# Two attention parts of a head pair placed by position over a whole period, and a PSUM bank for one of them

## The chip, the core and the metric

The kernel runs on one core of a Trainium2 chip, in one launch. The metric is the device time of that core in microseconds (us), the median of several runs. The engines are TensorE (PE, matmuls; its weight loads are shown as PEld), VectorE (DVE), ScalarE (ACT), GpSimd (POOL) and SyncE (SP), from which every DMA of this kernel is issued. Matmul results land in PSUM, which here is cut into eight banks of 128 x 512 fp32.

## What is computed

One step of a hybrid decoder layer, for 1024 prompt positions and 32 sample rows (8 requests of 4 tokens):

```python
z = rms_norm(x) @ w_in                       # 1056 x 2048 by 2048 x 7168
q, k, v, ga, u, vc, gb = split(z)            # 16 heads x 64; three gates and u, vc of width 1024
q, k = rope(q), rope(k)
oa = sum of three dilated windows of softmax attention, (128,1), (512,4), (2048,16), merged by denominators
vc = layer_norm(gelu(vc)); oc = gelu(u) * (masked 128x128 mixing of vc per group + bias)
y = rms_norm(x + concat(oa * silu(ga), oc * silu(gb)) @ w_out)
```

The prompt attends to itself; the sample attends to a cache of 2048 past positions, of which 896 per request are needed, and to its own 4 tokens. Keys, values and the normalised vc rows are outputs too.

## The kernel before, in words

**Precision.** Every fp32 operand of a matmul is split into a high and a low fp16 half (`hilo`, line 145; `w_split` for weights), and a product is three matmuls: high by high, high by low, low by high. So ACT makes each high half and DVE each low one.

**Projections.** The input projection has 56 tiles of 128 output columns, the output projection 16. A tile is 16 blocks of 128 deep, by three products, by three chunks of 352 rows: 144 matmuls on PE (`proj_chunk`, line 173). Its PSUM tiles come from the pool `ps_p` with three banks. A tile's weights are loaded two tiles ahead (`w_load`) and split one tile ahead, in four parts.

**Periods.** A head pair p needs the tiles v (values), x and y (queries and keys, whose two halves `rope` turns; `run_ab` runs both tiles chunk by chunk), g (its gate), and the loop adds u and b of the chunk group. Period p, from 1 to 8, is the run of tiles `g, u, b, v, x, y`: it has six tiles for p = 2 to 5 and five for p = 1, 6, 7 and 8. In it the projections of pair p run, and beside them the attention of pair g = p - 1.

**Steps beside a tile.** `proj_chunk` calls `fill` after every six matmuls: 24 calls a tile (`CALLS`). `fill` takes steps from a queue of (cost, function) and keeps their summed costs in proportion to the calls. A step only issues instructions; they go into the engines' streams there, and the scheduler of the language moves some of them by its own reckoning. Four lists of steps exist: the split of the next weights; `prompt_steps`; `sample_steps`; `mix_steps` (the chunk mixing).

**Prompt attention**, 16 items (8 query blocks by 2 heads), in 20 slots. Slot s issues for item s the scores (`fa`: PE into a bank of `ps_s`, a custom DVE reduce that adds the mask and finds the row's minimum, ACT's exp), for item s-1 the two halves of the probabilities (`fb`: ACT, DVE, and one DMA transpose on SP for each of up to two pieces, pn to pt), for item s-3 the product with the values (`fc`: PE into a bank of `ps_o`, then ACT and DVE), and in every second slot the gate (`gate`: a PE transpose into `ps_t`, then DVE and ACT).

**Sample attention**, per request (batch) a `prep` for keys and one for values: a load of 448 KB on SP into one of two buffers kvr, its high half kvh (ACT for keys, POOL for values), its low half kvl (DVE). `s_new` and `s_mm` are the scores: 7 key blocks by 2 small matmuls a batch. `soft1` transposes them in two groups of four blocks, each into its own `bank(ps_t)`, with the same custom reduce after each, then exp, sum and halves; it takes two of the three pn buffers. `soft2` transposes the probabilities by DMA (pst). `pv_new` and `pv_mm` are the products with the values, 14 small matmuls a batch, in one bank of `ps_o`. `fin` gates and stores the pair's result.

**Where they stand before.** The prompt's list is cut into pieces for the tiles g, u, b and v; the sample's first two loads are at the end of b's list, and all the rest of the sample runs beside x and y (in period 8 beside u and b of the last group). `wait(c)` is an empty step that only holds the queue back.

**PSUM before**: `ps_p` three banks, `ps_s` two, `ps_t` two, `ps_o` one. `ps_s` also takes the sample's scores, `ps_t` every PE transpose and the mixing (`mix`, whose result stays in its bank until DVE has made the low half chl), `ps_o` the sample's products.

Of the kernel before, what the change touches and what calls it, by code (L numbers as in the profile page):

```python
# [17 lines left out]
DB = 8  # L18
# [5 lines left out]
NP = H // 2  # L24
# [30 lines left out]
def hybrid_step_kernel(  # L55
# [40 lines left out]
    ps_s = pool("ps_s", bufs=2, space=PSUM)  # L96
    ps_t = pool("ps_t", bufs=2, space=PSUM)
    ps_o = pool("ps_o", bufs=1, space=PSUM)
# [6 lines left out]
    def bank(p, tag):  # L105
        return p.tile([128, 512], F32, tag=tag, name=tag)


# [44 lines left out]
    def set_steps(steps, ncalls):  # L153
# [5 lines left out]
        prog[2] = 0.0  # L159

    def fill():
# [105 lines left out]
    def x_tr(i, qd):  # L267
        t0, n = TILES[i]
        t = xn[i]
        p = bank(ps_s if qd % 2 else ps_t, "s" if qd % 2 else "t")  # L270
# [29 lines left out]
    def vc_sample(m0):  # L300
        p = bank(ps_t, "t")
        for j in range(4):
# [246 lines left out]
    def run_ab(p, steps):  # L549
        a, b = MA[p], MB[p]  # L550
        set_steps(steps, 2 * CALLS)
        for ci, (c0, n) in enumerate(CHUNKS):
# [6 lines left out]
            with tc.high_priority(offset=150):  # L559
                rope(p, pa, pb, c0, n)  # L560
        drain()
        stack_load()

# [31 lines left out]
    def prompt_steps(p):  # L595
# [91 lines left out]
        for s in range(n + 4):  # L687
            fs = []
            cost = 1.2 if s > 4 else 2.0
            if s - 4 >= 0 and (s - 4) % 2 == 1:  # L690
                fs.append(lambda t=(s - 4) // 2: gate(t))
            if 0 <= s - 3 < n:
                fs.append(lambda i=s - 3: fc(i))
                cost += 0.04 * (items[s - 3][0] + 1)
            if 0 <= s - 1 < n:
                fs.append(lambda i=s - 1: fb(i))
            if s < n:
                fs.append(lambda i=s: fa(i))
                cost += 0.04 * (items[s][0] + 1)
            slots.append((cost, lambda fs=fs: [f() for f in fs]))  # L700
        return slots, ahl

    def sample_steps(p, ahl):
# [97 lines left out]
        def pv_new():  # L801
            o = bank(ps_o, "o")
            cur["o"] = o
# [38 lines left out]

        pre = [(0.05, lambda: load(0)), (0.05, lambda: load(1))]
        s1 = [(0.1, lambda: prep(0)), (0.1, lambda: prep(1)), (0.2, s_new), wait(0.8)]
# [6 lines left out]
        return pre, s1, s2  # L851

# [71 lines left out]

    def cut(steps, fr):
        tot = sum(c for c, _ in steps)
        out, i, acc = [], 0, 0.0
        for f in fr:
            cur = []
            while i < len(steps) and (acc + steps[i][0] * 0.5 < f * tot or f >= 1.0):  # L930
                cur.append(steps[i])
                acc += steps[i][0]
                i += 1
            out.append(cur)
        return out

    def act_load(kts, c0, n):
# [4 lines left out]

    def head_start(pr):
        return [wait(1.5)] + pr

    def tail(p, steps):
        w_load(MB[p] + 1)
        for part in range(4):
            w_split(MB[p], part)
        run_ab(p, steps)  # L950

    for p in range(1, NP + 1):
        g = p - 1
        pr, ahl = prompt_steps(g)
        pre, s1, s2 = sample_steps(g, ahl)
        vs = lambda: spread(v_trs(p), 3)
        if p < NP - 2:
            mix_load(g)
            a2, a3, a4 = cut(pr[5:], (0.33, 0.67, 1.0))
            if g > 0:  # L960
                run_m(MG[g], head_start(pr[:5]), ga_evac)
            else:
                a2 = head_start(pr[:5]) + a2
            run_m(MU[g], a2, u_evac)
            run_m(MGB[g], a3 + pre, gb_evac)
            run_m(MV[p], merge(a4, mix_steps(g)), v_evac(p))
            tail(p, merge(s1 + s2, vs()))
        elif p == NP - 2:
            a2, a3 = cut(pr[5:], (0.5, 1.0))
            run_m(MG[g], head_start(pr[:5]), ga_evac)  # L970
            run_m(MU[g], a2 + pre, u_evac)
            run_m(MV[p], a3, v_evac(p))
            tail(p, merge(s1 + s2, vs()))
        elif p == NP - 1:
            mix_load(g - 1)
            a2, a3 = cut(pr[5:], (0.5, 1.0))
            run_m(MG[g], head_start(pr[:5]), ga_evac)
            run_m(MGB[g - 1], a2 + pre, gb_evac)
            run_m(MV[p], merge(a3, mix_steps(g - 1)), v_evac(p))
            tail(p, merge(s1 + s2, vs()))  # L980
        else:
            mix_load(g - 1)
            a2, a3, a4 = cut(pr[5:], (0.45, 0.9, 1.0))
            run_m(MG[g], head_start(pr[:5]), ga_evac)
            run_m(MU[g - 1], a2, u_evac)
            run_m(MGB[g - 1], a3 + pre, gb_evac)
            m = MU[g]
            w_load(m + 2)
            set_steps(mix_steps(g - 1) + merge(a4 + s1, split_steps(m + 1)), CALLS)
            for c0, n in CHUNKS:  # L990
                u_evac(proj_chunk(m, c0, n), c0, n)
            drain()
            mix_load(g)
            m = MGB[g]
            w_load(m + 2)
            set_steps(merge(s2, split_steps(m + 1)), CALLS)
            for ci, (c0, n) in enumerate(CHUNKS):
                gb_evac(proj_chunk(m, c0, n), c0, n)
                if ci == 2:
                    drain()  # L1000
                act_load(slice(0, 7), c0, n)
                act_load(slice(8, 15), c0, n)
            for c0, n in CHUNKS:
                act_load(slice(7, 8), c0, n)
            last_mix = mix_steps(g, direct=True)

# [53 lines left out]
    def ys_tr(m):  # L1060
        p = bank(ps_t, "t")
        PE.transpose(p[0:NS, 0:128], yts.pop(m), eye_t)  # L1062
# [3 lines left out]
    def y_tr(m, t0, w, sample=False):  # L1066
        p = bank(ps_t, "t")
        n = NS if sample else 128
# [230 lines left out]
```

## Time and profile before

| | |
|---|---|
| median of 3 runs | 1881.85 us (1880.05 to 1886.13) |
| the profiled execution: its own time | 1881.56 us |
| its span in the profile | 1879.8 us |
| granted clock of TensorE, mean | 0.995 |
| PE busy | 1790.0 us, 95% of the span |
| DVE, ACT, POOL busy | 58%, 39%, 7% |

A row of waits reads: engine, tile and line that waited, what it waited for, us in total, times, longest. A row of windows gives each engine's busy time and count in a stretch of the span, then the granted clock (1.00 is full), the DMA share and the rate. A row of the timeline gives start, duration, engine, line, operation, output and inputs. A row of a group gives the count, the busy time and the mean ns, then the idle time before it. The first period begins at 301.2 us and the last input tile ends at 1515.9 us.

### The profile page before, as it was taken

Reading aid. Unit: us, or ns where it says so; the run is one execution under the profiler, and the core shown is the slowest. Engines: PE = TensorE matmul, PEld = TensorE weight load, DVE = VectorE, ACT = ScalarE, POOL = GpSimd, SP = SyncE. Lnnn points to the kernel's source line nnn. Section 1 sums busy time; section 2 is a strip of 40 time slices with the busy share of each in tenths; the row PEclk is TensorE's granted clock in tenths of the full one; section 3 lists DMA queues with packets and bytes.
Section 4 is the critical chain, followed back from the end, with each engine's and each line's share of the span. In section 5 each row is a group of like instructions: output and inputs, shape, how many; then the busy total and the mean of one; then the engine's idle time right before and its main releaser. Section 6 shows DMA issues by size and latency. Waiting matters only on the chain. (4 is left out here: it accounts for less than half of the span.)

```text
span 1879.8 us, 37188 instructions
## 1 busy us (share of the span) xinstructions
PE 1790.0 (95%) x15040; PEld 1220.3 (65%) x15040; DVE 1085.5 (58%) x2392; ACT 724.5 (39%) x1605; POOL 125.2 (7%) x139
## 2 busy tenths in 40 slices
PE   8999998999999999999999999999989999999997
PEld 7866665666666666666666656666656666666667
DVE  7733696746665665665755566566566533324344
ACT  7522323632542453354244245245245311212134
POOL 0000010001001000100100100100100110000001
PEclk9999999999999999999999999999999999999999
DMA  7433346666656655656665666576675697222324
GB/s 260 118 81 68 81 135 184 122 166 172 147 117 180 180 120 162 191 115 154 172 157 125 160 202 116 149 210 130 165 197 110 178 336 190 68 68 68 77 59 185
DMA packets 340414, 276.13 MB, mean 147 GB/s; under 512 B 255889, under 2 KB 291729, under 8 KB 338129
## 3 DMA queue, kind: packets, MB, share of 16 engines
q1 hardware_dynamic: 340242, 273.76, 56.3%
q8 instruction: 117, 1.92, 0.4%
q14 instruction: 55, 0.45, 0.1%
HBM read 179.85 MB, written 38.26 MB: 116 GB/s over the span
## 5 line engine op out<-in xcount | busy, mean ns | idle before, releaser
L181 PE MATMUL proj<-xh,wh 128*128 128x352 f16 (+3 forms) x3712 | 1107.7, 303 | 6.2 <-DVE ta L475 2.9
L181 PE MATMUL proj<-xl,wh 128*128 128x352 f16 (+3 forms) x3712 | 1107.3, 303 | 1.5 <-DVE xl L147 1.5
L181 PE MATMUL proj<-xh,wl 128*128 128x352 f16 (+3 forms) x3712 | 1107.1, 303 | 0.4 <-DVE wl L139 0.4
L181 PEld LDWEIGHTS <-wh 128*128 128x128 f16 x7424 | 696.9, 98 | 325.4 <-issue 6.0
L181 PEld LDWEIGHTS <-wl 128*128 128x128 f16 x3712 | 362.6, 98 | 169.7 <-issue 1.9
L139 DVE SCALAR_TENSOR_TENSOR wl<-wraw,wh 128x512 f16<-128x512 f32 x288 | 202.3, 730 | 124.8 <-ACT wh L138 123.9
L138 ACT ACTIVATE wh<-wraw 128x512 f16<-128x512 f32 x288 | 165.8, 620 | 205.7 <-PE proj L181 198.7
L723 DVE SCALAR_TENSOR_TENSOR kvl<-kvr,kvh 128x896 f16<-128x896 f32 x128 | 143.0, 1117 | 95.3 <-ACT kvh L720 53.0
L632 ACT ACTIVATE sp<-sp,mn 128x256 f32<-128x256 f32 (+7 forms) x128 | 99.0, 773 | 150.6 <-DVE mn L620 150.6
L147 DVE SCALAR_TENSOR_TENSOR pn<-sp,pn 128x512 f16<-128x512 f32 (+2 forms) x192 | 106.4, 565 | 33.5 <-ACT pn L146 32.7
L722 POOL TENSOR_SCALAR kvh<-kvr 128x896 f16<-128x896 f32 x64 | 70.2, 1098 | 439.6 <-DMA kvr<-in_vc 272.2
L146 ACT ACTIVATE pn<-sp 128x512 f16<-128x512 f32 (+2 forms) x192 | 94.8, 516 | 11.4 <-DMA pt<-pn 8.4
L720 ACT ACTIVATE kvh<-kvr 128x896 f16<-128x896 f32 x64 | 60.7, 948 | 80.7 <-DMA kvr<-in_kc 46.4
L620 DVE CUSTOM_DVE_ANT_0 sp<-s,mp 128x512 f32<-128x512 f32 (+3 forms) x128 | 74.3, 584 | 21.6 <-PE s L612 20.1
L659 PE MATMUL o<-vst,pt 128*128 128x128 f16 x576 | 66.5, 220 | 21.0 <-DMA pt<-pn 17.4
L147 DVE SCALAR_TENSOR_TENSOR yhl<-proj,yhl 128x352 f16<-128x352 f32 (+1 forms) x42 | 21.4, 510 | 92.3 <-ACT yhl L146 92.3
L146 ACT ACTIVATE yhl<-proj 128x352 f16<-128x352 f32 (+1 forms) x42 | 18.8, 448 | 135.9 <-PE proj L181 116.5
L659 PEld LDWEIGHTS <-pt 128*128 128x128 f16 x576 | 52.1, 98 | 28.5 <-DMA pt<-pn 18.5
L639 DVE RECIPROCAL r<-den 128x1 f32<-128x1 f32 x128 | 20.8, 162 | 81.1 <-ACT sp L632 80.9
L666 PE MATMUL o<-vst,pt 128*128 128x64 f16 x576 | 63.0, 193 | 0.0
L923 POOL TENSOR_TENSOR gb<-gb,tb 128x352 f32<-128x352 f32 x24 | 28.8, 1201 | 511.4 <-DVE tb L203 511.4
L611 PE MATMUL s<-khd,qst 128*128 128x512 f16 (+2 forms) x192 | 61.7, 327 | 0.9 <-DVE mn L620 0.9
(165 smaller groups left out, 1562.6 us busy)
## 6 DMA issues: line engine op xcount, KB each, us to landing
wraw<-in_w_in SPq DMA_DIRECT2D x110, 512.0 KB, 4.5
kvr<-in_kc SPq DMA_DIRECT2D x64, 448.0 KB, 4.3
kvr<-in_vc SPq DMA_DIRECT2D x64, 448.0 KB, 4.0
wraw<-in_w_out SPq DMA_DIRECT2D x32, 512.0 KB, 5.1
yn<-in_x SPq DMA_DIRECT2D x8, 1024.0 KB, 9.2
out_y_p<-yn SPq DMA_DIRECT2D x16, 512.0 KB, 3.5
xn<-in_x SPq DMA_DIRECT2D x7, 1024.0 KB, 6.4
out_v_o<-tb SPq DMA_DIRECT2D x24, 176.0 KB, 2.5
```

The source lines that it names most:

```text
L138: ACT.activation(out=hi[:, sl, :], in_=r[:, rs, :], func=AF.Copy, scale=WS)
L139: DVE.scalar_tensor_tensor(out=lo[:, sl, :], in0=r[:, rs, :], scalar=WS, in1=hi[:, sl, :], op0=ALU.mult, op1=ALU.subtract)
L146: ACT.activation(out=hi, in_=src, func=AF.Copy, scale=scale)
L147: DVE.scalar_tensor_tensor(out=lo, in0=src, scalar=scale, in1=hi, op0=ALU.mult, op1=ALU.subtract)
L181: PE.matmul(out=ps[:, 0:n], lhsT=a[:, k, :], rhs=b[:, k, c0:c0 + n], start=(i == 0), stop=(i == 3 * KT - 1))
L611: PE.matmul(out=ps[:, 0:n], lhsT=qst[h][:, tq], rhs=khd[h][:, j0:j0 + n], start=True, stop=False)
L620: DVE.tensor_tensor_reduce(sp[:, j0:j0 + n], ps[:, 0:n], mp[:, S - nk + j0:S - nk + j0 + n], 1.0 / (QS * KS), prev, ALU.add, ALU.min, mn,)
L632: ACT.activation(out=sp[:, 0:nk], in_=sp[:, 0:nk], func=AF.Exp, scale=-1.0, bias=prev, accum_out=den)
L659: PE.matmul(out=o[:, 0:128].rearrange("p (l c) -> p l c", l=2), lhsT=pt[:, j], rhs=vst[:, :, kb, h * HD:(h + 1) * HD], start=(kb == 0), st ...
L666: PE.matmul(out=o[:, 0:64], lhsT=pt[:, w + j], rhs=vst[:, 0, kb, h * HD:(h + 1) * HD], start=False, stop=(kb == nb - 1))
L722: POOL.tensor_scalar(hi, r, VS, 1.0, ALU.mult, ALU.mult)
L723: DVE.scalar_tensor_tensor(out=lo, in0=r, scalar=KS if j < DB else VS, in1=hi, op0=ALU.mult, op1=ALU.subtract)
```

## The change

Costs and queues give way to positions. `period(p)` lists the period's tiles, n of them (x and y count as one each). Each step gets a time in tiles; `fill` advances a clock by 1/24 of a tile and issues all steps that are due. Prompt slots run from 0.65 to n - 0.85 (to n - 0.5 in the last period), spread by cost; the sample's events run over the whole period by given fractions of n, from 0.0 (first load) to 0.92 (`fin`); mixing runs from 0.15 to 1.6 tiles behind the start of v; weight splits at 0.15, 0.35, 0.55 and 0.75 of each tile; the transposes of the next pair's values at n - 0.6.

```diff
-    ps_t = pool("ps_t", bufs=2, space=PSUM)
+    ps_t = pool("ps_t", bufs=1, space=PSUM)
+    ps_v = pool("ps_v", bufs=1, space=PSUM)
...
+    def tbank():
+        flip[0] ^= 1
+        return bank(ps_t, "t") if flip[0] else bank(ps_v, "v")
...
     def fill():
+        if now[0] is not None:
+            now[0] += 1.0 / CALLS
+            while timeline and timeline[0][0] <= now[0]:
+                timeline.pop(0)[1]()
+            return
...
-            cost = 1.2 if s > 4 else 2.0
+            cost = 1.0
...
-            o = bank(ps_o, "o")
+            o = bank(ps_v, "v")
...
-                cur["s"] = bank(ps_s, "s")
+                cur["s"] = bank(ps_v, "v")
...
+        ev = [
+            (0.0, lambda: load(0)),
+            (0.02, lambda: load(1)),
+            (0.06, lambda: prep(0)),
+            (0.09, lambda: prep(1)),
+            (0.10, s_new),
+        ]
         for b in range(DB):
-            s1.append((0.4, lambda b=b: (s_mm(b), prep(b + 2))))
-        s2 = [wait(0.8), (0.4, soft1), wait(1.0), (0.4, soft2), wait(1.4), (0.1, pv_new)]
+            ev.append((0.13 + 0.035 * b, lambda b=b: (s_mm(b), prep(b + 2))))
+        ev += [(0.42, soft1), (0.46, soft2), (0.54, pv_new)]
         for b in range(DB):
-            s2.append((0.4, lambda b=b: (pv_mm(b), prep(DB + b + 2) if b < DB - 2 else None)))
-        s2.append((0.2, fin))
+            ev.append((0.545 + 0.047 * b, lambda b=b: (pv_mm(b), prep(DB + b + 2) if b < DB - 2 else None)))
+        ev.append((0.92, fin))
...
+        end = n - 0.85 if p < NP else n - 0.5
+        ev = at(pr, 0.65, end)
+        ev += [(t * n, f) for t, f in sample_steps(g, ahl)]
...
+                ev += at(mix_steps(mg), ready + 0.15, ready + 1.6)
...
+            ev += at(v_trs(p), end + 0.25, end + 0.5)
```

So the sample's scores and products use the bank v alone, the prompt keeps `ps_s` and `ps_o` for itself, and gates, mixing, `soft1` and the values' transposes share the single bank t. Outside the periods `tbank` takes t and v in turn.

In the rows below a name's number is the tile's running number. On PE, the sample's softmax of the fourth pair before (t_11631 and t_11638 are the two groups' banks, stsb the scores, wh and wl the weights' halves):

```order
L181 MATMUL proj_11591<-xh_81,wl_10996 128x352
L771 MATMUL t_11631<-eye_t_83,stsb_11310 64x128 x4
L771 MATMUL t_11638<-eye_t_83,stsb_11310 64x128 x3
L771 MATMUL t_11638<-eye_t_83,stsb_11310 64x32
L181 LDWEIGHTS wh_10995
```

And the same place now:

```order
L196 MATMUL proj_10727<-xh_84,wl_10231 128x352
L789 MATMUL t_10807<-eye_t_86,stsb_10054 64x128 x4
L196 LDWEIGHTS wh_10230
L196 MATMUL proj_10727<-xh_84,wh_10230 128x352
...
L196 LDWEIGHTS wl_10231
L196 MATMUL proj_10727<-xh_84,wl_10231 128x352
L789 MATMUL t_10814<-eye_t_86,stsb_10054 64x128 x3
L789 MATMUL t_10814<-eye_t_86,stsb_10054 64x32
```

Six projection matmuls now stand between the two groups. On DVE, around the reduces of the same softmax (ss<-t), before, with the sample's kvl, the rope (o12, qkhl, ta) beside it:

```order
L477 TENSOR_TENSOR o12_11570<-ta_11577,tb_11578 128x352
L723 SCALAR_TENSOR_TENSOR kvl_11565<-kvr_11507,kvh_11564 128x896
L147 SCALAR_TENSOR_TENSOR qkhl_11571<-o12_11570,qkhl_11571 128x704
L774 ISA ss_11630,mn_11636<-t_11631,msk_3650 64x512
L774 ISA mn_11636 64x1
L723 SCALAR_TENSOR_TENSOR kvl_11778<-kvr_11539,kvh_11777 128x896
L470 TENSOR_TENSOR ta_11722<-proj_11591,cos_t_2702 128x352
L774 ISA ss_11630,mn_11643<-t_11638,msk_3650,mn_11636 64x416
```

And now (sp and pn are a prompt item's scores and probabilities):

```order
L638 ISA sp_10775,mn_10779<-s_10776,mp_2709 128x512
L638 ISA mn_10779 128x1
L638 ISA sp_10775,mn_10784<-s_10781,mp_2709,mn_10779 128x128
L638 ISA mn_10784 128x1
L154 SCALAR_TENSOR_TENSOR pn_10866<-sp_10775,pn_10866 128x512
L792 ISA ss_10806,mn_10812<-t_10807,msk_3653 64x512
L792 ISA mn_10812 64x1
L792 ISA ss_10806,mn_10819<-t_10814,msk_3653,mn_10812 64x416
```

A prompt item's reduces and one of its low halves now stand ahead of the sample's reduces. On SP, a piece of the fourth pair's prompt stretch before (pt<-pn are the prompt's transposes, kvr the sample's loads, wraw weights):

```order
L648 DMA_TRANSPOSE pt_10268<-pn_10267 128x6x128
L120 DMA wraw_10516<-in_w_in 128x1024
L648 DMA_TRANSPOSE pt_10341<-pn_10340 128x8x128
L648 DMA_TRANSPOSE pt_10392<-pn_10391 128x8x128
L648 DMA_TRANSPOSE pt_10470<-pn_10469 128x8x128
L648 DMA_TRANSPOSE pt_10475<-pn_10474 128x2x128
```

And now:

```order
L730 DMA kvr_10448<-in_vc 128x896
L666 DMA_TRANSPOSE pt_10486<-pn_10485 128x6x128
L730 DMA kvr_10530<-in_vc 128x896
L666 DMA_TRANSPOSE pt_10570<-pn_10569 128x8x128
L730 DMA kvr_10621<-in_vc 128x896
L730 DMA kvr_10708<-in_vc 128x896
L666 DMA_TRANSPOSE pt_10664<-pn_10663 128x8x128
```

The sample's loads now stand between the prompt's transposes.

More of the change, by code (lines that the diff above doesn't have):

```diff
@@ L159, in set_steps @@
         prog[2] = 0.0
+    timeline = []
+    now = [None]
     def fill():
+        if now[0] is not None:
[3 more added lines that the diff above has]
+            return
         prog[0] += prog[1]
@@ L269, in x_tr @@
         t = xn[i]
-        p = bank(ps_s if qd % 2 else ps_t, "s" if qd % 2 else "t")
+        p = bank(ps_s, "s") if qd % 2 else tbank()
         for j in range(4):
@@ L300, in vc_sample @@
     def vc_sample(m0):
-        p = bank(ps_t, "t")
+        p = tbank()
         for j in range(4):
@@ L550, in run_ab @@
         a, b = MA[p], MB[p]
-        set_steps(steps, 2 * CALLS)
+        if steps is not None:
+            set_steps(steps, 2 * CALLS)
         for ci, (c0, n) in enumerate(CHUNKS):
@@ L561, in run_ab @@
         drain()
+        while timeline:
+            timeline.pop(0)[1]()
         stack_load()
@@ L693, in prompt_steps @@
                 fs.append(lambda i=s - 3: fc(i))
-                cost += 0.04 * (items[s - 3][0] + 1)
+                cost += 0.06 * (items[s - 3][0] + 1)
             if 0 <= s - 1 < n:
@@ L698, in prompt_steps @@
                 fs.append(lambda i=s: fa(i))
-                cost += 0.04 * (items[s][0] + 1)
+                cost += 0.06 * (items[s][0] + 1)
             slots.append((cost, lambda fs=fs: [f() for f in fs]))
@@ L801, in pv_new @@
         def pv_new():
-            o = bank(ps_o, "o")
+            o = bank(ps_v, "v")
             cur["o"] = o
@@ L923, in gb_evac @@
         POOL.tensor_tensor(out=gb[:, c0:c0 + n], in0=gb[:, c0:c0 + n], in1=b[:, 0:n], op=ALU.mult)
[L925 to L935, printed above, removed]
     def act_load(kts, c0, n):
@@ L941, in act_load, with at, period @@
             )
[L943 to L952, printed above, removed]
+    def at(steps, a, b):
+        tot = sum(c for c, _ in steps)
+        out, acc = [], 0.0
+        for c, f in steps:
+            out.append((a + (b - a) * acc / tot, f))
+            acc += c
+        return out
+    def period(p):
         g = p - 1
@@ L954, in hybrid_step_kernel @@
         pr, ahl = prompt_steps(g)
-        pre, s1, s2 = sample_steps(g, ahl)
-        vs = lambda: spread(v_trs(p), 3)
-        if p < NP - 2:
[L958 to L961, printed above, removed]
-            else:
[L963 to L987, printed above, removed]
-            w_load(m + 2)
[L989 to L1005, printed above, removed]
@@ new lines, in period @@
+        tiles = []
+        if g > 0:
+            tiles.append((MG[g], ga_evac))
+        if p < NP - 1:
+            tiles.append((MU[g], u_evac))
+        if p < NP - 2:
+            tiles.append((MGB[g], gb_evac))
+        if p == NP - 1:
+            tiles.append((MGB[g - 1], gb_evac))
+        if p == NP:
+            tiles += [(MU[g - 1], u_evac), (MGB[g - 1], gb_evac), (MU[g], u_evac), (MGB[g], gb_evac)]
+        n = len(tiles)
+        if p < NP:
+            tiles.append((MV[p], v_evac(p)))
+            n = len(tiles) + 2
@@ new lines, in period @@
+        end = n - 0.85 if p < NP else n - 0.5
+        ev = at(pr, 0.65, end)
+        ev += [(t * n, f) for t, f in sample_steps(g, ahl)]
+        mg = None
+        if p < NP - 2:
+            mg = g
+        elif p > NP - 2:
+            mg = g - 1
+        if mg is not None:
+            mix_load(mg)
+            if p < NP:
+                ready = len(tiles) - 1
+                ev += at(mix_steps(mg), ready + 0.15, ready + 1.6)
+            else:
+                ev += at(mix_steps(mg), 3.02, 3.3)
@@ new lines, in period @@
+        if p < NP:
+            ev += at(v_trs(p), end + 0.25, end + 0.5)
+        ev.sort(key=lambda e: e[0])
+        timeline.extend(ev)
+        now[0] = 0.0
+        for i, (m, evac) in enumerate(tiles):
+            w_load(m + 2)
+            last = p == NP and i == n - 1
+            if last:
+                mix_load(g)
+            sp = [(i + 0.15 + 0.2 * q, lambda q=q: w_split(m + 1, q)) for q in range(4)]
+            if p == NP or i < len(tiles) - 1:
+                timeline.extend(sp)
+            else:
+                timeline.extend([(i + 0.15 + 0.2 * q, lambda q=q: w_split(MA[p], q)) for q in range(4)])
+            timeline.sort(key=lambda e: e[0])
+            for ci, (c0, w) in enumerate(CHUNKS):
+                evac(proj_chunk(m, c0, w), c0, w)
+                if last:
+                    if ci == 2:
+                        while timeline:
+                            timeline.pop(0)[1]()
+                    act_load(slice(0, 7), c0, w)
+                    act_load(slice(8, 15), c0, w)
@@ L1008, in hybrid_step_kernel @@
+        if p < NP:
+            w_load(MB[p] + 1)
+            for q in range(4):
+                w_split(MB[p], q)
+            run_ab(p, None)
+        assert not timeline
+        now[0] = None
+        if p == NP:
+            for c0, w in CHUNKS:
+                act_load(slice(7, 8), c0, w)
+    for p in range(1, NP + 1):
+        period(p)
+    last_mix = mix_steps(NP - 1, direct=True)
     yt = {}
@@ L1060, in ys_tr @@
     def ys_tr(m):
-        p = bank(ps_t, "t")
+        p = tbank()
         PE.transpose(p[0:NS, 0:128], yts.pop(m), eye_t)
@@ L1066, in y_tr @@
     def y_tr(m, t0, w, sample=False):
-        p = bank(ps_t, "t")
+        p = tbank()
         n = NS if sample else 128
```

5 lines of the change are left out of this document (2 added, 3 removed).

## The prediction

> **What bounds the kernel now.** I read the page first: the share of each engine.
>
> ```profile
> span 1879.8 us, 37188 instructions
> PE 1790.0 (95%) x15040; PEld 1220.3 (65%) x15040; DVE 1085.5 (58%) x2392; ACT 724.5 (39%) x1605; POOL 125.2 (7%) x139
> ```
>
> TensorE (PE) is the bound, with 1879.8 - 1790.0 = 90 us in which it stands still. The change takes no matmul away, so it can only act on that time, on the clock, and on waits that it adds. Next I cut the span where the projection tiles begin: a stretch without attention, then the prompt stretch and the sample stretch of the first pair, and both of the fourth pair, a typical one.
>
> ```profile
> core 0: us, PE busy (x) PEld busy (x) DVE busy (x) ACT busy (x) POOL busy (x), PEclk, DMA share, GB/s
> 141.00:188.00 47.00, 47.00 (x317) 30.82 (x315) 14.46 (x29) 12.71 (x27) 0.00 (x0) 1.00 0.31 68
> 301.20:395.00 93.80, 83.73 (x662) 55.87 (x660) 56.41 (x160) 47.69 (x114) 3.62 (x5) 0.96 0.68 150
> 395.00:451.60 56.60, 50.64 (x513) 34.16 (x511) 33.69 (x50) 14.63 (x24) 7.64 (x7) 1.00 0.59 163
> 771.00:876.00 105.00, 103.31 (x819) 69.45 (x818) 66.61 (x182) 52.07 (x122) 4.49 (x6) 1.00 0.63 142
> 876.00:929.30 53.30, 50.47 (x513) 34.14 (x512) 32.94 (x50) 14.64 (x24) 7.81 (x7) 1.00 0.66 182
> ```
>
> Where projections run alone PE never stands and a matmul takes 47.00 / 317 = 0.148 us, so the projections have nothing to gain. The first pair loses 10.1 us beside the prompt and 6.0 beside the sample; the fourth 1.7 and 2.8. VectorE (DVE) is busy 60 to 63% in every stretch: spreading the work evenly does not make it a bound. Then the waits of PE alone, from the first pair's start to the end of the last input tile, which is all that the change touches:
>
> ```profile
> PE o L659 <- DMA pt<-pn: 17.4, 12, 4.9
> PE o L819 <- POOL kvh L722: 9.4, 7, 2.4
> PE o L808 <- DMA pst<-pn: 9.4, 8, 2.1
> PE s L751 <- ACT kvh L720: 7.9, 10, 1.8
> PE s L752 <- DVE kvl L723: 6.0, 7, 0.9
> PE o L820 <- DVE kvl L723: 5.5, 9, 0.7
> PE t L677 <- DVE onat L671: 4.7, 3, 1.7
> PE o L659 <- DVE onat L671: 1.7, 1, 1.7
> PE o L659 <- DVE sg L203: 1.6, 1, 1.6
> PE t L892 <- DVE chl L147: 1.1, 1, 1.1
> PE s L611 <- DVE mn L620: 0.9, 2, 0.5
> PE t L771 <- DVE stsb L759: 0.2, 1, 0.2
> ```
>
> They add up to 65.8 us. Five rows are the sample's (kvh, kvl, pst): 9.4 + 9.4 + 7.9 + 6.0 + 5.5 = 38.2. The prompt's transposed probabilities (pt) are 17.4. The last six come to 10.2.
>
> **The sample spread over the period.** A batch needs a load into one of two raw buffers and two conversions before the buffer is free:
>
> ```profile
> kvr<-in_kc SPq DMA_DIRECT2D x64, 448.0 KB, 4.3
> L720 ACT ACTIVATE kvh<-kvr 128x896 f16<-128x896 f32 x64 | 60.7, 948 | 80.7 <-DMA kvr<-in_kc 46.4
> L723 DVE SCALAR_TENSOR_TENSOR kvl<-kvr,kvh 128x896 f16<-128x896 f32 x128 | 143.0, 1117 | 95.3 <-ACT kvh L720 53.0
> ```
>
> That is 4.3 + 0.95 + 1.12 = 6.4 us over two buffers, one batch every 3.2 us. Before, 6 to 12 projection matmuls stand between two batches' score products in PE's order, 0.9 to 1.8 us; PE gets there first and waits. After, batches are 0.035 of a six-tile period apart, 0.21 of a tile's 144 matmuls or 4.5 us, in a five-tile period 0.175 or 3.7 us, and 0.047 (5.8 and 5.0 us) for values. All are over 3.2. The softmax's transposes get 0.08 of the period between them and the first value product, 10 us and more. So the 38.2 should fall to about 2: **-36 us** (bounds: -38, and -20 if the conversions queue behind the prompt's work).
>
> **The prompt.** Its slots run from 0.65 of the first tile until 0.85 before the end (0.5 in the last period). The same row for the first pair alone:
>
> ```profile
> PE o L659 <- DMA pt<-pn: 8.4, 3, 4.9
> ```
>
> Half of the 17.4 lies there; the longest, 4.9, is the first transposes behind the period's opening loads. Now the prompt starts 0.65 of a tile, 14 us, into the period, behind those loads, and smaller waits at other starts go the same way. But the transposes of probabilities now share buffers (three pn tiles, of which the sample's softmax takes two) and the SP queue with the sample. I keep 5 of the 17.4: **-12** (bounds -17 and +10). Of the other 10.2 I keep half, gates and sums being more widely spaced: **-5** (bounds -10 and 0).
>
> **The clock.** Two stretches of the region run at half clock:
>
> ```profile
> 314.30:321.10 6.80, 4.54 (x20) 2.52 (x21) 2.61 (x10) 1.75 (x6) 0.00 (x0) 0.50 0.73 189
> 1505.50:1508.90 3.40, 3.40 (x36) 1.99 (x33) 1.52 (x2) 0.47 (x1) 1.72 (x2) 0.50 1.10 381
> ```
>
> Half of 4.54 and of 3.40 is lost: 4.0 us. The first lies at the 4.9 us wait, the second behind a wait for pst; both waits go: **-4** (bounds -4 and +14, below). The second row follows a wait of at most 2.1 us, so short waits among the sample's thin products can cool the array; at worst each new wait beside the eight softmaxes costs another 1.7, 14 us. The Trainium skill, "TensorE: Matmul & The Clock Gate", section "Part 1: The HAM clock gate", ties the return to half clock to an idle window of about 3.4 us; by that no new wait of the size below would cool anything, and the trace does not bear the rule out here.
>
> **The wait that is added.** The t bank is single. The eight sample softmaxes each write two groups of transposes into t; before, all eight transposes ran in one go, now the second four stand behind the first reduce, with six projection matmuls (0.9 us) between. The row of PE and then those of DVE for the fourth pair before:
>
> ```profile
> 900.39 1.07 PE L771 MATMUL t<-eye_t,stsb 128*64 128x128 f32 x8
> ...
> 902.76 0.68 DVE L774 CUSTOM_DVE_ANT_0 ss<-t,msk 64x512 f32<-64x512 f32 x1
> 903.37 0.07 DVE L774 DVE_READ_ACCUMULATOR2_ANT mn<- 64x1 f32 x1
> ```
>
> The first four take half of the 1.07, until 900.9; the reduce is done at 903.4, 2.5 us later, because DVE has other work queued. Less 0.9 that is 1.6 us of stall; a DVE that stands ready would need 0.75 and no stall. After, DVE comes to the reduce through a prompt item's reduce, exp and low half, so it is not ready; I take 1.2, nearer the row: 8 x 1.2 = 10. While the transposes wait, every projection behind them in PE's queue waits, and nobody else gains. The other users of t are the gates and the mixing blocks. A mixing block holds its bank until its last reader is done:
>
> ```profile
> 867.68 0.22 PE L887 MATMUL t<-wm,vr 128*128 128x128 f16 x1
> ...
> 867.93 0.70 DVE L899 SCALAR_TENSOR_TENSOR t<-t,bb 128x512 f32<-128x512 f32 x1 [2.72 <-PE t L887]
> 868.98 0.69 DVE L900 TENSOR_TENSOR t<-t,gb 128x512 f32<-128x512 f32 x1
> 870.38 0.69 DVE L147 SCALAR_TENSOR_TENSOR chl<-t,chl 128x512 f16<-128x512 f32 x1 [0.71 <-ACT chl L146]
> ```
>
> From 867.9 to 871.1 is 3.2 us. In the order after, the next gate stands 18 projections and 16 attention products behind the block, about 3.7 us: little is left, but in the last period three hand-offs are closer. I take 8 us for all of them: in sum **+18** (bounds 0 and 50). The bank v of its own has 3.6 us or more of projections at each of its hand-offs, for two short readers: nothing.
>
> **The sum.** The profiled execution took 1881.56 us (span 1879.8), 0.3 under the median 1881.85, so no correction: 1881.6 - 36 - 12 - 5 - 4 + 18 = 1842.6, **1843 us**.
>
> **The rivals.** First, the hand-offs are free: DVE meets the reduce in time, the transposes are never late. 1843 - 18 - 5 = **1820**. For it speaks that DVE idles 40%; against it the 2.5 us in the rows above. Second, the hand-offs eat the gain: with both attentions feeding DVE, each reader of t comes 1.7 us later than its row. Then the softmaxes cost 8 x 3.3 = 26, sixteen mixing blocks 16 x (3.2 + 1.7 - 3.7) = 19, and three half-clock stretches 3 x 1.7 = 5: 50 in place of 18, and kvl is late too, 5: 1843 + 32 + 5 = **1880**, no change. It decides when DVE's backlog at a softmax passes about 2.5 us. The rule for it is in the Trainium skill, "PSUM — Partial Sum Buffer", section "Summary: rules for kernel authors": what is read while matmuls run should lie in a different bank. No run here shows yet what breaking it costs. Third, slower: SP issues in order, and waits for what each transfer needs:
>
> ```profile
> SPq L648 <- DVE pn L147: 196.4, 97, 4.0
> SPq L712 <- DVE kvl L723: 123.0, 77, 3.3
> ```
>
> In the order after, kvr loads stand between the prompt's transposes through most of the period; a load that waits for kvl delays the pt behind it. What a prompt item needs anyway, in rows:
>
> ```profile
> L147 DVE SCALAR_TENSOR_TENSOR pn<-sp,pn 128x512 f16<-128x512 f32 (+2 forms) x192 | 106.4, 565 | 33.5 <-ACT pn L146 32.7
> L146 ACT ACTIVATE pn<-sp 128x512 f16<-128x512 f32 (+2 forms) x192 | 94.8, 516 | 11.4 <-DMA pt<-pn 8.4
> L648 SPq DMA_TRANSPOSE pt<-pn x192: 1167/1232/2567, 313.3 to 1455.4; - x192
> pt<-pn SPq DMA_TRANSPOSE x192, 3.2
> ```
>
> High half, two low halves, the second issue and the landing: 0.52 + 2 x 0.57 + 1.23 + 3.2 = 6.1 us, and it has two slots. A tile with its attention takes 158.3 / 6 = 26.4 us; twenty slots over 4.5 tiles are 5.9 us each, in a five-tile period over 3.5 tiles 4.6. Two slots less 6.1 leave 5.7 and 3.1. Two loads per two slots at the mean wait of 123.0 / 77 = 1.6 us take 3.2: in the five-tile periods that is just the slack. With 1 us more per load each pair of slots there stretches by 2, each of 4 x 16 items by 1: 64 us, **1907**. It decides once the mean wait passes 1.6 us. Against it: those 77 waits come from stretches in which loads follow each other back to back, which the spacing ends. That the scheduler moves the steps back to where they were is excluded by the order, which shows them spread.
>
> **How the numbers follow.** Forecast 0.62, first rival 0.13, second 0.15, third 0.10. A run tells 0.3% or 5.6 us from no change: faster 0.62 + 0.13 + 0.05 of the second's lower side = 0.80, same 0.05, slower 0.05 + 0.10 = 0.15. The range from 1817 to 1872 takes in the first rival, the bounds of bank and clock, and leaves out the third and most of the second.
>
> **What would show it.** Right: the rows of PE for kvh, kvl and pst shrink to 2 or so; a new row, PE's softmax transposes waiting for mn, of 10 us in eight waits; pt under 8; the clock 1.00 near 316. The first five-tile period's idle time falls most. Wrong: pt rows above 30 us in the five-tile periods (third rival), softmax and gate rows together over 40 (second), or kvl rows that stay near 11, which would mean that DVE's order, not the loads, set the sample's pace.

## The result and the profile after

The changed kernel takes 1859.37 us (median of four runs, 1856.83 to 1859.98) against 1883.16 for the kernel before on the same chip (four runs); the ratio is 0.9871 with a 95% interval of 0.9852 to 0.9891. It is faster by 24 us where 39 were forecast, 16 us above the predicted 1843 and inside the range. The profiled execution took 1859.98 us. Its page:

```profile
span 1858.2 us, 37260 instructions
PE 1792.0 (96%) x15040; PEld 1228.3 (66%) x15040; DVE 1075.2 (58%) x2392; ACT 725.3 (39%) x1605; POOL 114.4 (6%) x139
```

PE stands still for 66 us instead of 90, and is busy 2 us longer with the same matmuls. The first period still begins at 301.2 us; the last input tile now ends at 1496.5. The waits of PE between the two, beside which the twelve rows of before are to be held:

```profile
PE t L695 <- DVE chl L154: 17.8, 9, 3.5
PE t L789 <- DVE mn L792: 8.7, 7, 2.8
PE t L695 <- DVE vss L537: 7.2, 4, 2.8
PE v L769 <- DVE stsb L758: 3.7, 1, 3.7
PE t L908 <- DVE af L698: 3.3, 1, 3.3
PE t L695 <- DVE onat L689: 1.8, 2, 1.0
PE o L677 <- DVE onat L689: 1.5, 1, 1.5
PE s L629 <- DVE mn L638: 0.2, 1, 0.2
```

Every row for kvh, kvl, pst and pt is gone: 38.2 + 17.4 = 55.6 us. What stands in their place are waits for the single bank t: 17.8 + 8.7 + 7.2 + 3.3 + 1.8 = 38.8 us. L695 is the gate's transposes, L789 the softmax's, L908 the mixing. The sum over all rows falls from 65.8 to 44.2.

Period by period, the fourth pair's (six tiles) and the sixth pair's (five tiles), first of before, then of after:

```profile
core 0: us, PE busy (x) PEld busy (x) DVE busy (x) ACT busy (x) POOL busy (x), PEclk, DMA share, GB/s
771.00:929.30 158.30, 153.78 (x1330) 103.59 (x1329) 99.55 (x231) 66.71 (x146) 12.30 (x13) 1.00 0.64 155
1089.70:1231.20 141.50, 131.54 (x1158) 87.84 (x1157) 88.78 (x213) 60.87 (x135) 8.72 (x10) 1.00 0.65 158
```

```profile
764.90:925.60 160.70, 154.88 (x1330) 104.30 (x1329) 97.51 (x231) 66.42 (x146) 11.04 (x13) 0.99 0.62 153
1085.60:1216.70 131.10, 129.97 (x1160) 88.59 (x1158) 86.66 (x213) 61.59 (x135) 8.50 (x10) 1.00 0.70 170
```

The five-tile period is 10.4 us shorter: PE's idle time falls from 10.0 to 1.1. The six-tile period is 2.4 us longer, its idle time goes from 4.5 to 5.8 and its busy time grows by 1.1. Taken together, the four five-tile periods take 552.9 us instead of 576.6 and the four six-tile ones 642.3 instead of 638.1 (their starts are those of the first tile of each): the gain was made in the former. The granted clock shows where some of the busy time comes from. Before, 10.2 us of the region ran at half clock; now there are 27.2 us, in seven stretches, of which these are three, and the sum of the seven:

```profile
410.10:413.50 3.40, 3.23 (x23) 2.37 (x24) 3.26 (x11) 0.86 (x3) 0.00 (x0) 0.50 0.57 95
696.80:700.20 3.40, 3.40 (x20) 2.09 (x21) 2.88 (x8) 0.51 (x2) 0.00 (x0) 0.51 0.56 153
1321.50:1324.90 3.40, 3.40 (x25) 2.23 (x23) 3.40 (x9) 1.41 (x3) 0.00 (x0) 0.50 0.48 76
...
sum 27.20, PE 25.04 PEld 16.09 DVE 24.72 ACT 9.19 POOL 0.93; mean PE 3.58 PEld 2.30 DVE 3.53 ACT 1.31 POOL 0.13
```

If a matmul takes twice as long at half clock, half of the 25.04 us of matmuls there is lost: an estimate of 12.5 us, where it was 4.0 before.

**One wait followed back.** The longest gate wait, at 696.7 us, in the timelines of PE, DVE, ACT and SP:

```profile
696.74 0.37 PE L695 MATMUL t<-eye_t,onat 128*128 128x128 f32 x1 [3.54 <-DVE chl L154]
```

```profile
690.47 0.74 DVE L154 SCALAR_TENSOR_TENSOR pn<-sp,pn 128x512 f16<-128x512 f32 x1
695.42 0.56 DVE L154 SCALAR_TENSOR_TENSOR pn<-sp,pn 128x384 f16<-128x384 f32 x1 [4.22 <-ACT pn L153]
695.90 0.69 DVE L154 SCALAR_TENSOR_TENSOR chl<-t,chl 128x512 f16<-128x512 f32 x1
```

```profile
689.80 0.63 ACT L153 ACTIVATE pn<-sp 128x512 f16<-128x512 f32 x1
694.87 0.52 ACT L153 ACTIVATE pn<-sp 128x384 f16<-128x384 f32 x1 [4.44 <-DMA pt<-pn]
695.29 0.58 ACT L153 ACTIVATE chl<-t 128x512 f16<-128x512 f32 x1
```

```profile
685.85 1.53 SPq L127 DMA_DIRECT2D wraw<-in_w_in  x2
687.49 2.59 SPq L666 DMA_TRANSPOSE pt<-pn  x2
```

Read from the top: PE waits until DVE has read the mixing block out of t. That reading, chl, has no quarrel with the bank; it stands in DVE's queue behind the low half of a prompt item's probabilities, which waits 4.22 us for ACT's high half. ACT waits 4.44 us for a pn buffer: all three hold probabilities whose transposes have not landed. The one it waits for was issued at 687.49 and landed 7.4 us later, twice the median of 3.6; before it SP had waited 4.9 us for wl, until 685.85, to issue a weight load that stands ahead of it. So a shortage of buffers at ACT is passed on by two queues that run in order to a matmul that has nothing to do with it, and the single bank t is only where it comes out. In the groups of the page:

```profile
L154 DVE SCALAR_TENSOR_TENSOR pn<-sp,pn 128x512 f16<-128x512 f32 (+2 forms) x192 | 114.9, 608 | 70.5 <-ACT pn L153 69.7
L153 ACT ACTIVATE pn<-sp 128x512 f16<-128x512 f32 (+2 forms) x192 | 96.9, 518 | 52.4 <-DMA pt<-pn 47.3
pt<-pn SPq DMA_TRANSPOSE x192, 3.6
```

ACT's wait for the buffers was 8.4 us before and is 47.3; DVE's for ACT was 32.7 and is 69.7. A buffer is also held longer: from the start of the n-th high half on ACT to the end of the n-th transposing issue on SP the mean over the 192 pieces is 4.06 us, against 3.41 before. The landing, counted from the start of the issue, takes 3.6 against 3.2 (medians). From the high half to the landing it is 6.6 against 5.5 us in the mean, over the 170 and 166 pieces whose landing is on record.

### The profile page after: what moved, and what is told of

Same layout as the page of the kernel before. It is cut to its first block, busy times and chain, and to the rows that moved or that the text cites. A ratio compares the mean times of both kernels' runs of the same rounds, so it can differ in the third digit from the quotient of the medians.

```text
span 1858.2 us, 37260 instructions
## 1 busy us (share of the span) xinstructions
PE 1792.0 (96%) x15040; PEld 1228.3 (66%) x15040; DVE 1075.2 (58%) x2392; ACT 725.3 (39%) x1605; POOL 114.4 (6%) x139
## 5 line engine op out<-in xcount | busy, mean ns | idle before, releaser
L146 DVE SCALAR_TENSOR_TENSOR wl<-wraw,wh 128x512 f16<-128x512 f32 x288 | 190.4, 690 | 134.2 <-ACT wh L145 133.7
L154 DVE SCALAR_TENSOR_TENSOR pn<-sp,pn 128x512 f16<-128x512 f32 (+2 forms) x192 | 114.9, 608 | 70.5 <-ACT pn L153 69.7
L153 ACT ACTIVATE pn<-sp 128x512 f16<-128x512 f32 (+2 forms) x192 | 96.9, 518 | 52.4 <-DMA pt<-pn 47.3
L740 POOL TENSOR_SCALAR kvh<-kvr 128x896 f16<-128x896 f32 x64 | 63.7, 995 | 835.1 <-DVE r L657 340.0
L153 ACT ACTIVATE yhl<-proj 128x352 f16<-128x352 f32 (+1 forms) x42 | 18.8, 446 | 124.3 <-PE proj L196 95.5
L688 ACT ACTIVATE ot<-o,r 128x64 f32<-128x64 f32 x128 | 39.1, 305 | 68.8 <-PE o L684 68.2
L630 PE MATMUL s<-klo,qst 128*128 128x512 f16 (+2 forms) x192 | 61.3, 332 | 0.0
```

Source lines behind the costliest of these rows:

```text
L146: DVE.scalar_tensor_tensor(out=lo[:, sl, :], in0=r[:, rs, :], scalar=WS, in1=hi[:, sl, :], op0=ALU.mult, op1=ALU.subtract)
L153: ACT.activation(out=hi, in_=src, func=AF.Copy, scale=scale)
L154: DVE.scalar_tensor_tensor(out=lo, in0=src, scalar=scale, in1=hi, op0=ALU.mult, op1=ALU.subtract)
L740: POOL.tensor_scalar(hi, r, VS, 1.0, ALU.mult, ALU.mult)
```

## The experiments

Two theories went into the first four. **B**: the hand-offs of the single bank t by themselves took the 39 us that were forecast down to 24. **Q**: DVE is late because ACT waits for pn buffers; the bank only passes it on. All are edits of the changed kernel unless it is said otherwise, and times are medians of four runs, where no other number is given, with the ratio to the kernel before on the same chip (medians of 1881 to 1883 us).

**e1_softv**: the second group of the softmax's transposes goes to bank v, which is free then.

```diff
-                pt = bank(ps_t, "t")
+                pt = bank(ps_v, "v") if g else bank(ps_t, "t")
```

> The second group of the sample softmax's transposes goes to the bank v, free at that time, instead of waiting for t. Theory B (the gain was eaten at the hand-offs of the single bank t): the row of PE's softmax transposes waiting for mn, 8.7 us in seven waits, goes; nothing else changes, the seven half-clock stretches stay, since they lie at gates behind mixing blocks: 1850 us, 9 under the changed kernel's 1859. Theory Q (DVE is late because ACT waits for pn buffers whose transposes are stuck in SP's queue; the bank only passes that on): the same wait goes from PE, but the late reduce delays the prompt item behind it, and a part comes back as waits for onat or pt: 1853 to 1857.

Measured: 1859.96 us, ratio 0.9873 (0.9853 to 0.9893): no gain. The mn row is gone, but the gates' row has grown by more:

```profile
PE t L695 <- DVE chl L154: 28.9, 9, 5.9
```

The wait moved on to the next user of t; ACT's wait for pn stayed at 47.8 us. Both theories had expected some gain; B's, the larger, failed by the more.

**e2_mixsb**: the mixing's result goes to SBUF, so that t is free after DVE's first step instead of its last.

```diff
-        cf = pm
+        cf = ap_.tile([128, 512], F32, tag="vr", name="mcf", bufs=2)
...
-        DVE.scalar_tensor_tensor(out=o3, in0=o3, scalar=1.0 / (VRS * SWS), in1=bias, op0=ALU.mult, op1=ALU.add)
+        c3 = cf.rearrange("p (a b) -> p a b", a=4) if part < 2 else cf[:, 0:n]
+        DVE.scalar_tensor_tensor(out=c3, in0=o3, scalar=1.0 / (VRS * SWS), in1=bias, op0=ALU.mult, op1=ALU.add)
```

> The mixing block's first DVE step writes to SBUF (into the slot of the vr tile it has used up) instead of back into t, so t is free after one step of 0.7 us, not after the low half chl. Theory B: gates behind mixing blocks no longer wait: the rows of 17.8 and 7.2 us fall under 4 together, the block that waited 3.3 stays, and most of the 27 us at half clock go, which cost 12: 1859 - 21 - 11 = 1827. Theory Q: DVE still stands 4 us at a time behind ACT's pn, so the wait moves to the gate's own inputs, to onat and pt; waits fall by about 12 and the clock by half: 1841.

Measured: 1859.79 us, ratio 0.9862 (0.9835 to 0.9888). No gain again:

```profile
PE t L695 <- DVE mcf L923: 14.6, 6, 4.5
PE t L789 <- DVE mn L792: 9.2, 7, 2.5
PE t L695 <- DVE onat L689: 8.5, 6, 2.7
```

The gates wait for whatever DVE reads next, 23.1 us in two rows where it was 26.8 in three, and half clock in the region grew from 27.2 to 40.9 us. So it is DVE's lateness more than how long the mixing holds the bank.

**e3_pn4**: four pn buffers instead of three. One of the three kvl buffers makes room for it.

```diff
-                pn = ap_.tile([128, 1024], F16, tag="pn", name="pn", bufs=3)
+                pn = ap_.tile([128, 1024], F16, tag="pn", name="pn", bufs=4)
...
-            lo = ap_.tile([128, NKEY], F16, tag="kvl", name="kvl", bufs=3)
+            lo = ap_.tile([128, NKEY], F16, tag="kvl", name="kvl", bufs=2)
...
-            pn = cur["pn"] = [ap_.tile([128, 1024], F16, tag="pn", name="pn", bufs=3) for _ in range(2)]
+            pn = cur["pn"] = [ap_.tile([128, 1024], F16, tag="pn", name="pn", bufs=4) for _ in range(2)]
```

> A fourth pn buffer (room from the third kvl buffer, two left). Banks as in the changed kernel. Theory Q: ACT's waits of pn for the DMA pt, 47 us, fall under 20, DVE's longest stands go, and the gates wait for chl half as long, so 28 us of gate waits fall to 14 and half of the half-clock time goes: 1859 - 14 - 6 = 1839. Theory B: the hold of t, 3.2 us by DVE's and ACT's own durations, is what is longer than the matmuls between; gates wait as before: 1856 to 1862.

Measured: **1827.26 us**, ratio 0.9697 (0.9675 to 0.9719), 32 us below the changed kernel. The page, PE's first rows and ACT's row of waits:

```profile
span 1824.9 us, 37222 instructions
PE 1780.9 (98%) x15040; PEld 1224.9 (67%) x15040; DVE 1088.0 (60%) x2392; ACT 723.3 (40%) x1605; POOL 125.6 (7%) x139
```

```profile
PE t L789 <- DVE mn L792: 9.4, 8, 2.3
PE v L769 <- DVE stsb L758: 4.4, 1, 4.4
PE t L695 <- DVE vss L537: 3.0, 4, 0.8
```

```profile
ACT pn L153 <- DMA pt<-pn: 3.6, 4, 1.4
```

With the same banks, ACT's wait falls from 47.3 to 3.6, the gates' 17.8 us behind chl from the first place to 0.5, and half clock in the region from 27.2 to 3.4 us. Of the 33 us of span, 22 are idle time of PE (66 to 44) and 11 are busy time (1792.0 to 1780.9); half of the 23.8 us of half clock that went is 12. B falls as the main cause. Q had put 14 us on the waits and 6 on the clock; both came out larger.

**e4_bankonly** starts from the kernel before: one bank t, and bank v for the sample's scores and products, with everything else placed as before.

```diff
-    ps_t = pool("ps_t", bufs=2, space=PSUM)
+    ps_t = pool("ps_t", bufs=1, space=PSUM)
+    ps_v = pool("ps_v", bufs=1, space=PSUM)
...
-            o = bank(ps_o, "o")
+            o = bank(ps_v, "v")
...
-                cur["s"] = bank(ps_s, "s")
+                cur["s"] = bank(ps_v, "v")
...
-            o = bank(ps_o, "o")
+            o = bank(ps_v, "v")
```

> The bank split alone in the old placement: t single, the sample's scores and products in v, prompt and sample apart as before. Theory B: softmax hand-offs cost 8 x 1.6 = 13 us and gates behind mixing blocks some 5, so slower than before by 18: 1901. Theory Q: in the old placement ACT hardly waits for pn (8 us), DVE is in time, and only the softmaxes pay: slower by 5 to 10: 1890.

Measured: 1895.17 us (five runs), ratio 1.0060 (1.0038 to 1.0083): 12 us slower.

```profile
PE o L660 <- DMA pt<-pn: 20.1, 12, 6.1
PE t L772 <- DVE mn L775: 9.5, 7, 3.0
PE v L753 <- DVE kvl L724: 6.5, 7, 0.9
PE v L820 <- POOL kvh L723: 6.3, 8, 1.9
PE v L752 <- ACT kvh L721: 5.2, 10, 1.8
```

The rows of t sum to 18.8 us (the softmax's 9.5, and 9.3 in five others), where before they were 6.0: in this placement, where the prompt's buffers are not short, the single bank adds 12.8 us of waits, and the prediction had put down 18. The sample's rows are 23.7 us with its own bank, 38.2 before: the bank ends a part of them, the larger part stays. So PE's idle time is nearly as before, 1896.1 - 1804.2 = 91.9 us, and the loss is in its busy time, 1804.2 against 1790.0, with 30.6 us of half clock in the region against 10.2. The time lies between what B and Q gave and does not decide between them.

**e5_kvl2** is the other half of e3_pn4: two kvl buffers, three pn.

> The changed kernel with two kvl buffers in place of three, and nothing else; it is the other half of e3_pn4, in which a fourth pn buffer was paid for with a kvl buffer. Theory Q (pn buffers): the 32 us of e3_pn4 came from the pn buffer, so this stays at 1857 to 1863, ACT's pn waits for the transposes stay near 47 us and half clock near 27 us. The rival theory K: it was the kvl buffer (loads held back, so that the sample's transfers keep out of the way of the prompt's transposes in SP's queue): then this is 1825 to 1835 and the fourth pn buffer did nothing.

Measured: 1854.96 us, ratio 0.9859 (0.9843 to 0.9875). The rival falls: of the 32 us, at most a few come with the kvl buffer (1859.4 - 1855.0 = 4, but the intervals of the two ratios to the kernel before overlap, so even these are not certain). ACT still waits 35.8 us for pn. Four pn buffers beside three kvl were not tried.

**e6_pn4softv** is e3_pn4 with the edit of e1_softv.

> e3_pn4 with the softmax's second group of transposes in bank v (the edit of e1_softv). With ACT no longer held back, PE's 9.4 us of waits for mn are the largest row left. Theory Q: with the lateness gone nothing takes the place of those 9.4, so 1816 to 1820. Theory B said that the bank's hand-offs cost by themselves, and gives the same here; the rival is that the waits move on once more, as in e1_softv, to gates or scores behind the softmax: 1825 to 1829.

Measured: 1826.82 us, ratio 0.9708 (0.9694 to 0.9723), as e3_pn4. The 9.4 us behind mn are gone; 5.7 us of gates behind chl and a second half-clock stretch (10.2 us in the region instead of 3.4) came for them. The rival was right.

**e7_bpn4** is the kernel before with four pn and two kvl buffers.

> The kernel before, with four pn buffers and two kvl buffers, and nothing else. Theory Q as the cause of the missing gain: before, ACT waits only 8.4 us for the transposes and DVE 40 us for pn, so the buffer was not scarce in the old placement; with one kvl buffer fewer, the sample beside x and y may wait 0 to 10 us more: 1873 to 1893, not faster than before by more than 8 us. The rival: the pn buffers were scarce in either placement (the 17.4 us of pt waits of PE), and the gain of 32 us has nothing to do with the change: 1845 to 1865.

Measured: 1893.70 us, ratio 1.0068 (1.0050 to 1.0086): 12 us slower than before, just above what Q gave. In the old placement the fourth buffer brings PE's waits for pst from 9.4 to 3.2 us, those for pt hardly change (16.4, 17.4 before), and those for the keys' kvh grow from 7.9 to 14.6. PE's idle time stays, 1891.4 - 1801.9 = 89.5 us; the loss is in its busy time, 1801.9 against 1790.0, with 34 us of half clock in the region instead of 10.2. Which of the two buffers causes that, the run does not say. The same exchange of buffers that costs 12 us here became worth 32 through the change.

**e8_poolload** moves the sample's loads from SP's queue to GpSimd's.

```diff
-            SP.dma_start(out=t, in_=src[p, :, j % DB])
+            POOL.dma_start(out=t, in_=src[p, :, j % DB])
```

> The changed kernel with the sample's kvr loads issued from GpSimd's queue instead of SP's, so that no transpose stands behind a load that waits for kvl. It asks why three pn buffers were too few. Theory Q1: the transposes were late because SP issues in order and the loads and weights stand ahead of them; with the 64 loads and their 108 us of waits for kvl out of SP's queue, the transposes land earlier, ACT's pn waits fall from 47 to below 15 us, and the time to 1830 to 1842. Theory Q2: three buffers, of which the sample takes two for its softmax, are too few however early the transposes are issued: ACT's pn waits stay above 35 us and the time at 1855 to 1862. GpSimd's issue itself may cost: the kvh of the values stand behind the loads there, which would show as PE waits for kvh, 5 to 15 us.

Measured: 1865.58 us (1858.44 to 1867.66), ratio 0.9918 (0.9902 to 0.9935): slower than the changed kernel by some 6 to 9 us. The profile is of the fastest of the four runs. ACT's wait falls only from 47.3 to 39.5, as Q2 said, and Q1 falls for these loads:

```profile
ACT pn L153 <- DMA pt<-pn: 39.5, 27, 4.9
```

The landing of a pt does not become shorter (median 4.0 us, 3.6 in the changed kernel). In SP's queue the weight loads, which wait 87.4 us for wl in the changed kernel (44.8 before), still stand ahead of transposes, as at 685.85 above. To move those was not tried.

**e9_pns** divides the buffers: two pn for the prompt, two for the sample's softmax, two kvl.

```diff
-                pn = ap_.tile([128, 1024], F16, tag="pn", name="pn", bufs=3)
+                pn = ap_.tile([128, 1024], F16, tag="pn", name="pn", bufs=2)
...
-            lo = ap_.tile([128, NKEY], F16, tag="kvl", name="kvl", bufs=3)
+            lo = ap_.tile([128, NKEY], F16, tag="kvl", name="kvl", bufs=2)
...
-            pn = cur["pn"] = [ap_.tile([128, 1024], F16, tag="pn", name="pn", bufs=3) for _ in range(2)]
+            pn = cur["pn"] = [ap_.tile([128, 1024], F16, tag="pns", name="pns", bufs=2) for _ in range(2)]
```

> The changed kernel with the pn buffers divided: two for the prompt alone, two of the sample's softmax's own, kvl two instead of three; the same room as e3_pn4, but not shared. It asks for whom three were too few. Theory Q2: the sample's softmax, which takes two of the three and holds them until its own transposes have landed, starves the prompt; divided, the prompt never meets it, so ACT's pn waits fall below 15 us and the time is 1825 to 1833, like e3_pn4. Theory Q3: a prompt item by itself needs three buffers at the new pace (two pieces an item, each held for about 6 us by its transposes), so two are too few all through the period: ACT's pn waits above 47 us and the time 1855 to 1885.

Measured: 1860.79 us, ratio 0.9878 (0.9847 to 0.9910).

```profile
ACT pn L153 <- DMA pt<-pn: 60.4, 40, 5.0
```

So it is not only that the sample takes two of three: two buffers that the prompt has to itself are too few (Q3). The same room shared, in e3_pn4, is enough.

**e10_squeeze** is e3_pn4 with the sample's events in the last two tiles of the period.

```diff
-        ev += [(t * n, f) for t, f in sample_steps(g, ahl)]
+        ev += [(n - 2 + 2 * t, f) for t, f in sample_steps(g, ahl)]
```

> e3_pn4 (1827) with the sample's events put back into the period's last two tiles (their fractions count over two tiles instead of the period), the prompt staying where the change put it. It measures the step of the prediction that was worth -36. Theory of that step: batches are then 0.07 of a tile, 1.7 us, apart, below the 3.2 us that a batch needs, so PE's waits for kvh, kvl and pst return with 20 to 35 us, DVE has both attentions in the same two tiles, and the time is 1850 to 1870. The rival: the sample's own bank v, not the spread, ended those waits, since PE no longer shares a bank between them: 1827 to 1838.

Measured: 1878.86 us (ten runs), ratio 0.9989 (0.9969 to 1.0008): 52 us above e3_pn4, and all that the change gained over before is gone.

```profile
PE v L826 <- DMA pst<-pn: 12.1, 8, 2.4
PE v L769 <- DVE stsb L777: 9.1, 6, 2.5
PE t L789 <- DVE stsb L777: 6.5, 7, 2.0
PE v L838 <- DVE kvl L741: 4.0, 10, 0.9
PE v L837 <- POOL kvh L740: 3.6, 6, 1.7
```

The sample's waits return: 11.8 us for kvh and kvl, 12.1 for pst, and another 15.6 for stsb, where e3_pn4 has 4.4 for stsb and nothing for the others. This is with a bank of its own: the spread, and not the bank, is what ended them. The time is 9 us above the theory's range, since the waits for stsb and 23.8 us of half clock (3.4 in e3_pn4) were not in it.

**e11_start** is e3_pn4 with the prompt's slots from 0.1 of the first tile on.

```diff
-        ev = at(pr, 0.65, end)
+        ev = at(pr, 0.1, end)
```

> e3_pn4 (1827) with the prompt's slots starting at 0.1 of the first tile of a period instead of 0.65. It measures the step of the prediction that was worth -12. Theory of that step: the first transposes stand behind the period's opening loads, so PE waits for pt again, 8 to 15 us in all, most at the starts of periods: 1833 to 1845. The rival: the start does not matter, the evenly spread slots do, and with more room between slots the waits fall further: 1820 to 1829.

Measured: 1847.18 us (1841.81 to 1851.53), ratio 0.9812 (0.9787 to 0.9836): 20 us above e3_pn4.

```profile
PE t L789 <- DVE mn L792: 18.9, 7, 3.5
PE o L677 <- DMA pt<-pn: 5.9, 3, 5.3
```

Waits for pt do return, 5.9 us in three where 8 to 15 were expected; more comes from the softmax, whose waits for mn grow from 9.4 to 18.9 us, and from 20.4 us of half clock. The late start is right, but only a part of its worth is the reason that was given for it.

**e12_best** has the fourth pn buffer and both edits that relieve t.

> e6_pn4softv (1827) with the mixing's result written to SBUF, the edit of e2_mixsb: both edits that take readers off the bank t, with the fourth pn buffer. Left of waits for the bank t in e6_pn4softv are 5.7 us of gates and 1.8 and 1.1 us of mixing behind chl. If the bank's hand-offs still cost by themselves, these 8 go: 1817 to 1821. If, with pn on time, what is left is only the order in which DVE gets to its work, they move to another row: 1824 to 1829.

Measured: **1821.41 us** (1819.57 to 1825.68), ratio 0.9679 (0.9661 to 0.9698), the fastest here: 60 us under before, 38 under the changed kernel.

```profile
PE t L695 <- DVE onat L689: 8.0, 4, 2.9
PE v L769 <- DVE stsb L758: 3.6, 1, 3.6
```

Against e6_pn4softv it gains 5 us, near what was expected if hand-offs still cost; the intervals of the two ratios touch, so this last step is not certain.

## Why the prediction came out as it did

The sign and the mechanism of the gain held: the waits that the spread should end are gone. The time lies in the range in part by luck: the waits for t and the clock came 30 us dearer than forecast, and 5 more from pt and 8.5 that no row explains made up for almost half of it. The terms against the profiled executions, in us, as forecast and as measured:

| term | forecast | measured |
|---|---|---|
| sample's waits (kvh, kvl, pst; after: stsb) | -36 | 3.7 - 38.2 = -34.5 |
| prompt's waits for pt | -12 | -17.4 |
| rows of t: new hand-offs, and those of the other six | +18 and about -3 | 38.8 - 6.0 = +32.8 |
| other rows of o and s | about -2 | 1.7 - 4.2 = -2.5 |
| clock | -4 | 12.5 - 4.0 = +8.5 |
| no row | 0 | -8.5 |
| sum | -39 | -21.6 |

- **The sample spread over the period** was right in size and cause: the rows vanish, the bank of its own alone leaves 23.7 of the 38.2 (e4_bankonly), and squeezing the sample together again brings 23.9 back (e10_squeeze).
- **The prompt** gained more than the -12. The late start does what was said of it, but in e11_start the waits for pt are only 5.9 of 20 us.
- **The single bank t, +18, is the step that was mis-sized.** Its first part was right: 10 us in eight softmax waits were forecast, 8.7 in seven came, and 9.5 in the old placement (e4_bankonly). The second part, 8 us for gates and mixing, came to 17.8 + 7.2 + 3.3 + 1.8 = 30.1. I took the time for which a mixing block holds t, 3.2 us, from a row in which DVE waited 0.71 us before its last step. After the change that last step stood up to 4.2 us behind a prompt's low half.
- **Its reason stood in the prediction, at the wrong place.** It said that the pn buffers and SP's queue are now shared and put that into the bounds of the prompt's own products (up to +10). Those products no longer wait for pt at all. The shortage shows where the buffer is written, on ACT, and then at PE instructions that come through DVE.
- **The clock, -4,** failed with it. The stretch near 316 did go, but seven others came, 12.5 us instead of none. The bound of +14 had the right picture, half clock behind short waits, but put it beside the softmaxes; six of the seven stand at a gate's wait and one, at 1437.5 us, at the mixing's wait of 3.3. With the fourth pn buffer all but 3.4 us of half clock go (e3_pn4).
- **The signs.** As said, kvh, kvl, pst and pt went, the softmax's row came, and the clock near 316 is 1.00. It was not the first five-tile period whose idle time fell most: it fell from 16.0 to 8.5 us, the sixth pair's from 10.0 to 1.1. Slips in the working move no term: 0.047 of a six-tile period is 6.0 us and not 5.8, 0.08 of a five-tile one is 8.5 at the same pace and not 10, and the 5 us that the first rival takes off beside the 18 are not derived.
- **The rivals.** Of the second, softmax and gate waits together, 35.5 us, came near its 40, and its picture of a late DVE is what happened; its cause, the hand-offs of the bank, is not what mattered: relieving them changed nothing while pn was short (e1_softv, e2_mixsb), and some 5 us, not certain, when it no longer was (e12_best). The third is not there as it was told: no product waits for pt, and taking the loads out of SP's queue does not help (e8_poolload). The Trainium skill's rule, "PSUM — Partial Sum Buffer", section "Summary: rules for kernel authors", to read another bank than the one that is written, gets a price from e4_bankonly, where one bank less for the hand-offs added 12.8 us of waits (18.8 - 6.0). The rule does not tell whether a bank or its reader is short.

**Open.** Why three pn buffers no longer do is settled as to what mends it, not as to what does it. A longer hold of each buffer (6.6 against 5.5 us from high half to landing), the two that the softmax takes, and the weight loads in SP's queue all point the same way, and no run has each alone. The fourth buffer does not shorten the hold, which is 7.0 us in e3_pn4; it lets ACT go on in the meantime. The -8.5 us in no row are not explained either: 6.5 of them are busy time of PE, which grew by 2.0 us where the clock alone would have added 8.5, and 2.2 lie outside the region (1879.8 - 1214.7 = 665.1 before, 1858.2 - 1195.3 = 662.9 after).

## What to carry to other kernels

When two streams of work are laid beside each other, count the staging buffers that they share, and price a shortage at the engine that fills the buffer and at everything queued behind it there, not at the reader. A wait that names a PSUM bank is followed back through DVE and ACT before the bank is blamed: here taking readers off the bank gave nothing, and one more buffer in SBUF, 2 KB in each partition, in place of another one, gave 32 us. A stall among thin matmuls (those of 128 columns or fewer) should be priced with the clock that it may cost as well: 12.5 of the changed kernel's 1858 us, by the estimate above.

## What was not expected of the hardware

A gate's wait of 1.91 us was enough to be followed by a stretch at half clock, while a wait of 3.67 us at 319.7 us was not:

```profile
1321.16 0.33 PE L695 MATMUL t<-eye_t,onat 128*128 128x128 f32 x1 [1.91 <-DVE chl L154]
```

```profile
319.74 0.17 PE L769 MATMUL v<-qbd,kvh 128*128 128x16 f16 x1 [3.67 <-DVE stsb L758]
```

Two other gate waits, of 2.47 us at 1018.5 and 2.16 us at 1038.5, were not followed by one either. So the length of the single wait does not decide it. The Trainium skill, "TensorE: Matmul & The Clock Gate", section "Part 1: The HAM clock gate", has the clock fall after an idle window of about 3.4 us that runs freely; the length of the stretches, 3.4 us or twice that, agrees, the idle time needed does not.
